# Decays of rows 512 to 1023 in two groups of two heads, the second group in z_a's last two products

## The chip, the cores and the metric

The kernel runs on one core of one Trainium2 chip. The metric is the device time in microseconds (us) of one execution. Before the change it is 1072.09 us, the median of 3 runs (1071.81 to 1072.77).

A core has engines that run side by side, each with a queue of its own that is worked off in order: TensorE (PE, matmuls into the PSUM banks), VectorE (DVE), ScalarE (ACT), GpSimd (POOL) and SyncE (SP, which here only issues DMAs). An instruction waits on semaphores for what other engines or DMAs have to finish first.

## The reference, cut to what matters

One layer of a decoder trunk on 1024 rows of width 1024: a norm, one wide projection cut into parts, gated linear attention with four heads, a gated short convolution, a merge and an output projection. The part that the change touches is the decay of the attention:

```python
proj = jnp.einsum('bsd,dc->bsc', h, w_in[i])
(q, k, v, z_a, gk_low, cb, cc, xc, z_c, g_a, g_c) = jnp.split(proj, idx, axis=-1)
gk = jax.nn.log_sigmoid((jnp.einsum('bsr,rk->bsk', gk_low, w_gk2[i]) + b_gk[i]).astype(jnp.float32)) / GATE_NORMALIZER
...
b = jnp.cumsum(gk, axis=3)
b_last = b[:, :, :, -1:, :]
q_in = q * jnp.exp(b)
k_in = k * jnp.exp(-b)
k_dec = k * jnp.exp(b_last - b)
decay = jnp.exp(b_last[:, :, :, 0, :])
...
y_a = jnp.einsum('bsv,vd->bsd', o * jax.nn.silu(z_a), w_branch_a[i])
```

## The kernel before

**Products.** Each large matrix product is done by a scheme with seven products of half-size blocks instead of eight, in float32 split into a high and a low part; each block product is three matmuls, hi x hi, lo x hi and hi x lo. The projections of v and of z_a are made by `wide`: here six products, in the order 3, 1, 2, 5, 4, 6. Each runs over four k-tiles `kt` and four row blocks `b`, three matmuls a time: 48 matmuls of 128x512, which add into four PSUM banks. Product 3 goes into the set X, product 1 into V, product 2 into Y, product 5 into V, products 4 and 6 into Y again. For z_a, X and Y are the banks m4, m5, o, o, and V is m0 to m3 (for v it is the other way round, so m0 to m3 are free for z_a's V once v's last results have been read). In the names, zaX, zaV and zaY are these banks; za1hi and za1lo are the weights of product 1, h1hi and h1lo its rows; zas, zau and sz are results on their way to the silu and to the store szd.

After product 5, DVE adds V to the copies zau (this frees V's banks); after product 4 it adds Y to the copies zas, before product 6 adds to the same banks.

**Decays.** `low_rank` makes the gate's low-rank rows for one half of the rows; `decays` then makes per head one matmul zp of 128x512 into a bank, reads it twice on ACT (Relu into a tile c, Abs into a tile t), then takes Exp and Ln of t on ACT (these, and the silu, need different function tables, so ACT_TABLE_LOAD stands between them), adds c on DVE, sums along the rows with a scan, subtracts the last row of each chunk, and stores both (ccd and cdd). A small Exp (dcs) and a product (dds) give the chunk's decay. The tiles t and c have four buffers each, which `quarter_sums` uses as well, for tiles named qs that are stored to tqd and loaded back later as turned0.

For the half that the change concerns (rows 512 to 1023), `more` runs `decays` for four heads and then `quarter_sums`; it is woven into z_a's products (`weave`, `tick`): after every second row block the generator is asked for its next step. `weights`, which prepares later weights (wt, wtd), is woven in beside it.

**What sets the order.** The program is recorded first and then put in order, engine by engine, by a list scheduler with costs of its own and due times. Matmuls of the main products keep their order; zp and the low-rank matmuls are side work that the scheduler slots in. `hurry` makes an instruction's due time earlier, `apart` asks for a distance from what it depends on. All instructions are issued from one line (L508), so views of the profile are read by the names of the tiles.

Of the kernel before, what the change touches and what calls it, by code (L numbers as in the profile page):

```python
# [9 lines left out]
F32 = mybir.dt.float32  # L10
# [509 lines left out]
def kernel(  # L520
# [42 lines left out]
    bgk = vec[:, 0:4]  # L563
# [8 lines left out]
    def dram(name, *shape):  # L572
        return dr.tile([P, *shape], F32, name=name)
# [5 lines left out]
    cd = [[[dram(f"c{w}d{h}_{i}", HALF) for w in "cd"] for i in range(2)] for h in range(H)]  # L579
# [16 lines left out]
    store = nc.sync.dma_start  # L596
# [6 lines left out]
    def mm(*a, **kw):  # L603
        nc.tensor.matmul(*a, skip_group_check=True, **kw)
# [12 lines left out]
    def weave(gen, after=1):  # L617
        woven.append([after, gen])
# [11 lines left out]
    def finish_woven():  # L630
        while woven:
            tick()
# [334 lines left out]
    def pairs(cs):  # L967
        for c in cs:
            c.prods = [k for k in PAIR if k in c.prods]
        return [list(cs[n:n + 2]) for n in range(0, len(cs), 2)]  # L970

    def run_groups(groups, more=(), ahead=6):


        todo = line_up(groups)
        seq = todo + line_up(more)
        for n, (c, k) in enumerate(todo):
            for reach, what in ((RING + ahead, "load"), (RING - 1, "prep")):
# [498 lines left out]
    with phase("v", [ph["prep0"]]) as qp:  # L1477
# [14 lines left out]
        smask = qp.tile([P, HALF], F32, name="smask")  # L1492
# [17 lines left out]
        nbgk = qp.tile([P, 4], F32, name="nbgk")  # L1510
# [20 lines left out]
                tt(low[a:a + 32], lowp[a:a + 32], f(low[a:a + 32]), op=ALU.subtract)  # L1531
            lows[half] = low

        def decays(half, tags):
            t1 = [qp.tile([P, HALF], F32, tag="t1", name=f"t1_{half}{h}", bufs=4) for h in range(H)]
            c = [qp.tile([P, HALF], F32, tag="c4", name=f"c4_{half}{h}", bufs=4) for h in range(H)]
            for h in range(H):
                zp = pso.tile([P, 512], F32, tag=tags[h], name=f"zp{half}_{h}", bufs=2 if tags[h] == "o" else 1)
                cs = slice(h * P, (h + 1) * P)
                nc.apart = 1.0  # L1540
                mm(zp, g2[:, cs], lows[half], start=True, stop=True)
                nc.apart, nc.hurry = 0.0, 6.0
                act(c[h], zp, AF.Relu, scale=-1.0, bias=nbgk[:, h:h + 1])
                act(t1[h], zp, AF.Abs, bias=bgk[:, h:h + 1])
                nc.hurry = 0.0
                yield 1
            for t in t1:
                act(t, t, AF.Exp, scale=-1.0)
            for t in t1:
                act(t, t, AF.Ln, bias=1.0)  # L1550
            yield 1
            by = lambda t: t.rearrange("p (n c t) -> p n c t", c=2, t=CH)
            for h in range(H):
                tt(t1[h], t1[h], c[h], op=ALU.add)
                nc.vector.tensor_tensor_scan(c[h], smask, t1[h], 0.0, op0=ALU.mult, op1=ALU.add)
                store(cd[h][half][0], c[h])
                last = by(c[h])[:, :, :, CH - 1]
                tt(by(t1[h]), by(c[h]), by(c[h])[:, :, :, CH - 1:CH].to_broadcast([P, NP, 2, CH]), op=ALU.subtract)
                store(cd[h][half][1], t1[h])
# [44 lines left out]
        def extra():  # L1604
            low_rank(0)
            yield 2
            yield from decays(0, ("o",) * 4)
            low_rank(1)

        def more():  # L1610
            yield from decays(1, ("m0", "m1", "m2", "m3"))
            yield from quarter_sums(1)

        wide("v", [wv[0, n] for n in range(4)], v_cons, ("m0", "m1", "m2", "m3"), ("o", "o", "m4", "m5"),
             [(ep, "ev", 3)] * 2, [(ep, "ev", 3), (qp, "t1", 4)], begun, lambda: weave(extra(), 1))
        weave(more(), 1)
        weave(weights(qp, pieces[:3], 3, 5.0), 2)
        wide("za", [wv[1, n] for n in range(4)], z_cons, ("m4", "m5", "o", "o"), ("m0", "m1", "m2", "m3"),
             [(qp, "vhi", 2)] * 2, [(qp, "vlo", 2)] * 2)
        finish_woven()  # L1620
        qks = []
        for hp in range(2):
# [367 lines left out]
    with phase("late", [ph["sw"], ep]) as lp:  # L1990
# [57 lines left out]
        with phase("fin", [ph["sw4"]], lp) as gp:  # L2048
# [152 lines left out]
            last = pairs(gts)  # L2201
# [74 lines left out]
```

## Time and profile before

| | us |
|---|---|
| median of 3 runs | 1072.09 |
| profiled execution | 1072.38 |
| its span | 1070.5 |
| mean granted clock of TensorE | 0.998 of full speed |

The span runs from the first to the last record of the profiled execution; 1.9 us lie around it. Times of instructions are microseconds from the start of the span. z_a's first product begins near 168, its second at 178.26, product 2 at 191.16, product 5 at 202.04 and product 4 at 212.92 in the chain of work that ended last (the chain counts a piece from the release of its first instruction; the timeline of PE has starts some 0.16 us earlier). After product 6, at 234.68, the cells of q and k begin (q0V, k0V, q0X, k0X).

How to read the rows: a row of the timeline has the start, the length, the engine, the line, the operation, what it writes and reads, and in brackets how long the engine stood idle before it, with the releaser. PE's matmuls overlap: one of 0.39 us follows the other after 0.23 us. A row of the windows has busy time per engine, with the number of instructions, then the granted clock, the DMA share and GB/s.

### The profile page before, as it was taken

To read this page: it belongs to the slowest core of one execution; us is meant where nothing else is said; L and a number is where in the kernel's file an instruction comes from. 1 tells how busy PE (TensorE), PEld (TensorE's weight loads), DVE (VectorE), ACT (ScalarE), POOL (GpSimd) and SP (SyncE) were. 2 spreads that over 40 slices of the span, in tenths; PEclk is the share of its full clock that TensorE was granted. 3 is DMA by queue.
4 is the path that set the end of the run, shared out by engine and by line. 5 is a ranking of instruction groups with operands and counts; after the bars stand their busy time and mean duration, and the time that the engine had idled before them with its cause. 6 is when DMAs were issued, how large, how long until landed. Compare 5 with 4: busy or idle time off the path is not lost.

```text
span 1070.5 us, 15921 instructions
## 1 busy us (share of the span) xinstructions
PE 1059.7 (99%) x5175; PEld 896.3 (84%) x5175; DVE 917.5 (86%) x1553; ACT 662.8 (62%) x1241; POOL 45.4 (4%) x83
## 2 busy tenths in 40 slices
PE   9999999999999999999999999999999999999996
PEld 7888887888888888888888888888888888888886
DVE  6889768977997888889889788887999879889896
ACT  6866689856654544566556376765856635466555
POOL 0000000000000000000000011110000000012021
PEclk9999999999999999999999999999999999999999
DMA  9985578785867443654557779978586779799973
GB/s 313 330 316 174 187 231 307 260 285 200 257 213 244 154 152 130 215 173 154 197 180 243 247 241 346 324 275 322 199 305 229 284 220 312 244 328 337 300 235 133
DMA packets 166979, 262.06 MB, mean 245 GB/s; under 512 B 14448, under 2 KB 79728, under 8 KB 163952
## 3 DMA queue, kind: packets, MB, share of 16 engines
q1 hardware_dynamic: 166752, 260.79, 72.1%
q8 instruction: 40, 0.66, 0.2%
q14 instruction: 43, 0.35, 0.1%
q10 hardware_dynamic: 144, 0.26, 0.1%
HBM read 168.72 MB, written 92.27 MB: 244 GB/s over the span
## 4 chain that ended last, share of the span: by engine, by line
PE 98%; ACT 1%; DMA 1%; DVE 0%; issue 0%; SPq 0%; POOL 0%; POOLq 0%; ACTq 0%
PE vY L508 3%; PE zaY L508 3%; PE vV L508 2%; PE op L508 2%; PE zaV L508 2%; PE pe L508 2%; PE zaX L508 1%; PE vzV L508 1%; PE vzX L508 1%; PE kv L508 1%; PE ga1Y L508 1%; PE ga0Y L508 1%; PE k0Y L508 1%; PE zc2Y L508 1%; PE zc1Y L508 1%; PE ga2Y L508 1%
## 5 line engine op out<-in xcount | busy, mean ns | idle before, releaser
L508 DVE TENSOR_TENSOR wt<-wt 128x256 f32<-128x256 f32 x64 | 26.9, 420 | 2.2 <-DMA wtd<-wt 1.9
L508 ACT ACT_TABLE_LOAD x20 | 25.7, 1283 | 1.1 <-PEq L2265 0.7
L508 DVE SCALAR_TENSOR_TENSOR u<-t,vec,u 128x512 f32<-128x512 f32 x32 | 23.8, 747 | 2.6 <-ACT u L508 2.5
L508 ACT ACTIVATE junk<-x 128x512 bf16<-128x512 f32 (+1 forms) x30 | 18.0, 600 | 12.0 <-DVE x L508 11.7
L508 POOL MEMSET t<- 128x2 f32 x8 | 0.8, 100 | 410.3 <-ACT kk L508 206.5
L508 POOL TENSOR_SCALAR rg<-ms 128x1 f32<-128x1 f32 x8 | 6.4, 798 | 261.6 <-ACT junk L508 261.4
L508 ACT ACTIVATE u<-t,vec 128x512 f32<-128x512 f32 x16 | 11.6, 726 | 7.9 <-issue 4.6
L508 ACT ACTIVATE junk<-op 128x256 bf16<-128x256 f32 x32 | 12.2, 380 | 3.8 <-PE op L508 3.7
L508 ACT ACTIVATE wt<-wt,vec 128x256 f32<-128x256 f32 x32 | 13.6, 497 | 1.0 <-DMA wt<-in_wb_dram 1.0
L508 ACT ACTIVATE og<-op,or 128x256 f32<-128x256 f32 x32 | 13.3, 470 | 1.2 <-POOL or L508 1.1
L508 ACT CAST S<-S 128x512 fp32r<-128x512 f32 x14 | 8.6, 617 | 8.7 <-PE op L508 7.5
L508 PE MATMUL pe<-wpehi,pThi 128*128 128x512 f32 x32 | 12.7, 398 | 0.6 <-ACT pThi L508 0.5
L508 ACT ACTIVATE oq<-oq,vec 128x512 f32<-128x512 f32 x20 | 13.1, 715 | 0.0
L508 PE MATMUL op<-v,aTh 128*128 128x256 f32 x64 | 12.8, 283 | 0.0
L508 PE MATMUL pe<-wpelo,pThi 128*128 128x512 f32 x32 | 12.7, 398 | 0.0
L508 DVE TENSOR_TENSOR szl<-og,szl 128x512 f32<-128x512 f32 x16 | 11.0, 687 | 2.0 <-ACT og L508 2.0
L508 PE MATMUL pe<-wpehi,pTlo 128*128 128x512 f32 x32 | 12.1, 393 | 0.0
L508 POOL TENSOR_TENSOR or<-or,mhalf 128x2 f32<-128x2 f32 x16 | 11.9, 746 | 1.3
L508 DVE SCALAR_TENSOR_TENSOR hq<-hq,vec,rt 128x512 f32<-128x512 f32 x16 | 11.4, 741 | 0.0
L508 DVE TENSOR_TENSOR s<-y,s 128x512 f32<-128x512 f32 x16 | 11.0, 686 | 0.5 <-ACT s L508 0.5
L508 POOL TENSOR_SCALAR or<-oms 128x2 f32<-128x2 f32 x16 | 5.6, 348 | 137.6 <-ACT junk L508 137.6
L508 DVE TENSOR_TENSOR x<-x,pe 128x512 f32<-128x512 f32 (+1 forms) x18 | 11.2, 629 | 0.3
(3671 smaller groups left out, 4333.7 us busy)
## 6 DMA issues: line engine op xcount, KB each, us to landing
wtd<-wt SPq DMA_DIRECT2D x88, 128.0 KB, 2.7
wt<-in_wb_dram SPq DMA_DIRECT2D x16, 512.0 KB, 4.5
v<-vd SPq DMA_DIRECT2D x16, 512.0 KB, 5.9
wgq<-wtd SPq DMA_DIRECT2D x7, 1024.0 KB, 6.6
qk<-qkd SPq DMA_DIRECT2D x12, 512.0 KB, 6.0
vraw<-in_wv_dram SPq DMA_DIRECT2D x20, 256.0 KB, 3.3
zaraw<-in_wv_dram SPq DMA_DIRECT2D x20, 256.0 KB, 4.4
uq<-ud SPq DMA_DIRECT2D x5, 1024.0 KB, 6.9
```

Of the source, the lines that this page charges most:

```text
L508: o.call(*[place(a) for a in o.args], **{k: place(a) for k, a in o.kw.items()})
```

## The change

`decays` now takes the heads that it is to make, and loops over them. `more` makes heads 0 and 1 only, in the banks m0 and m1, and then the quarter sums. Heads 2 and 3 are made by a second generator, in the banks m2 and m3, which z_a's `wide` starts by its hook `late`: after the weights of product 6 have been prepared and before the matmuls of product 4 are recorded. The hook was there before (v's `wide` uses it); z_a's did not use it.

```diff
-        def decays(half, tags):
-            t1 = [qp.tile([P, HALF], F32, tag="t1", name=f"t1_{half}{h}", bufs=4) for h in range(H)]
-            c = [qp.tile([P, HALF], F32, tag="c4", name=f"c4_{half}{h}", bufs=4) for h in range(H)]
-            for h in range(H):
-                zp = pso.tile([P, 512], F32, tag=tags[h], name=f"zp{half}_{h}", bufs=2 if tags[h] == "o" else 1)
+        def decays(half, heads, tags):
+            t1 = [qp.tile([P, HALF], F32, tag="t1", name=f"t1_{half}{h}", bufs=4) for h in heads]
+            c = [qp.tile([P, HALF], F32, tag="c4", name=f"c4_{half}{h}", bufs=4) for h in heads]
+            for n, h in enumerate(heads):
+                zp = pso.tile([P, 512], F32, tag=tags[n], name=f"zp{half}_{h}", bufs=2 if tags[n] == "o" else 1)
...
-            for h in range(H):
-                tt(t1[h], t1[h], c[h], op=ALU.add)
+            for n, h in enumerate(heads):
+                tt(t1[n], t1[n], c[n], op=ALU.add)
...
-                yield from decays(0, ("o",) * 4)
+                yield from decays(0, range(4), ("o",) * 4)
...
         def more():
-            yield from decays(1, ("m0", "m1", "m2", "m3"))
+            yield from decays(1, range(2), ("m0", "m1"))
             yield from quarter_sums(1)
...
         wide("za", [wv[1, n] for n in range(4)], z_cons, ("m4", "m5", "o", "o"), ("m0", "m1", "m2", "m3"),
-             [(qp, "vhi", 2)] * 2, [(qp, "vlo", 2)] * 2)
+             [(qp, "vhi", 2)] * 2, [(qp, "vlo", 2)] * 2, None, lambda: weave(decays(1, range(2, 4), ("m2", "m3")), 1))
```

No matmul is added or taken away: PE has 5000 rows in both orders, with the same operations. ACT has four rows more, which are table loads (24 for 20 in the program). What follows are three places in the order; zp_2 and zp_3 are the matmuls of heads 2 and 3, and the number behind a name is that of a buffer.

**Place 1: from product 3 to product 1 of z_a, on PE.** Before, ending in the first matmuls of zaV:

```order
L508 MATMUL zaX_1748<-za3hi_1822,h3lo 128x512
L508 MATMUL zp_2_1984<-low_1742,g_1407 128x512
L508 MATMUL zaX_1784<-za3hi_1822,h3hi 128x512
L508 MATMUL zaX_1784<-za3lo_1847,h3hi 128x512
L508 MATMUL zaX_1784<-za3hi_1822,h3lo 128x512
L508 MATMUL zaX_1815<-za3hi_1822,h3hi 128x512
L508 MATMUL zaX_1815<-za3lo_1847,h3hi 128x512
L508 MATMUL zaX_1815<-za3hi_1822,h3lo 128x512
L508 MATMUL zaV_2000<-za1hi_1864,h1hi 128x512
L508 MATMUL zp_3_2004<-low_1742,g_1407 128x512
L508 MATMUL zaV_2000<-za1lo_1880,h1hi 128x512
L508 MATMUL zaV_2000<-za1hi_1864,h1lo 128x512
```

and in the changed kernel:

```order
L508 MATMUL zaX_1669<-za3hi_1763,h3lo 128x512
L508 MATMUL zaX_1775<-za3hi_1763,h3hi 128x512
L508 MATMUL zaX_1775<-za3lo_1830,h3hi 128x512
L508 MATMUL zaX_1775<-za3hi_1763,h3lo 128x512
L508 MATMUL zaX_1843<-za3hi_1763,h3hi 128x512
L508 MATMUL zaX_1843<-za3lo_1830,h3hi 128x512
L508 MATMUL zaX_1843<-za3hi_1763,h3lo 128x512
L508 MATMUL zaV_1990<-za1hi_1795,h1hi 128x512
L508 MATMUL zaV_1990<-za1lo_1851,h1hi 128x512
L508 MATMUL zaV_1990<-za1hi_1795,h1lo 128x512
L508 MATMUL zaV_1999<-za1hi_1795,h1hi 128x512
```

Both zp are gone from here; zaV follows on zaX.

**Place 2: the first row blocks of product 4, on PE and on ACT.** PE before, the third and fourth row block:

```order
L508 MATMUL zaY_2044<-za4lo_2220,h4hi 128x512
L508 MATMUL zaY_2044<-za4hi_2204,h4lo 128x512
L508 MATMUL zaY_2048<-za4hi_2204,h4hi 128x512
L508 MATMUL zaY_2048<-za4lo_2220,h4hi 128x512
L508 MATMUL zaY_2048<-za4hi_2204,h4lo 128x512
L508 MATMUL zaY_2062<-za4hi_2204,h4hi 128x512
L508 MATMUL zaY_2062<-za4lo_2220,h4hi 128x512
L508 MATMUL zaY_2062<-za4hi_2204,h4lo 128x512
```

and now:

```order
L508 MATMUL zaY_2022<-za4hi_2167,h4hi 128x512
L508 MATMUL zaY_2022<-za4lo_2190,h4hi 128x512
L508 MATMUL zaY_2022<-za4hi_2167,h4lo 128x512
L508 MATMUL zaY_2031<-za4hi_2167,h4hi 128x512
L508 MATMUL zp_2_2372<-low_1747,g_1407 128x512
L508 MATMUL zaY_2031<-za4lo_2190,h4hi 128x512
L508 MATMUL zaY_2031<-za4hi_2167,h4lo 128x512
L508 MATMUL zp_3_2378<-low_1747,g_1407 128x512
L508 MATMUL zaY_2081<-za4hi_2167,h4hi 128x512
L508 MATMUL zaY_2081<-za4lo_2190,h4hi 128x512
L508 MATMUL zaY_2081<-za4hi_2167,h4lo 128x512
```

zp_2 stands behind the first matmul of zaY's third block, zp_3 behind its last. On ACT, what stood between the last cast of product 6's weights (za6hi) and the casts of q0 and k0 before:

```order
L508 CAST za6hi_2385<-zaT_1695 128x512
L508 CAST qs12h<-qs_2345 128x512
L508 ACT_TABLE_LOAD
L508 ACTIVATE zau_2258<-zau_2258 128x512
L508 ACTIVATE zau_2270<-zau_2270 128x512
L508 CAST q0hi<-q0T_2431 128x512
```

and now:

```order
L508 CAST za6hi_2359<-zaT_1703 128x512
L508 ACT_TABLE_LOAD
L508 ACTIVATE zau_2229<-zau_2229 128x512
L508 ACTIVATE t_12_2380<-zp_2_2372,vec 128x512
L508 ACTIVATE c_12_2387<-zp_2_2372,nbgk 128x512
L508 ACTIVATE t_13_2393<-zp_3_2378,vec 128x512
L508 ACTIVATE c_13_2398<-zp_3_2378,nbgk 128x512
L508 ACT_TABLE_LOAD
L508 ACTIVATE t_12_2380<-t_12_2380 128x512
L508 ACTIVATE t_13_2393<-t_13_2393 128x512
L508 ACT_TABLE_LOAD
L508 ACTIVATE t_12_2380<-t_12_2380 128x512
```

The reads of zp_2 and zp_3, two Exp and two Ln, with two more table loads, (the second Ln, of t_13, follows the last row shown) stand between the first zau's silu and the second's.

**Place 3: from product 4 to the cells of q and k, on DVE and on SP.** DVE before, around the sums zas that free zaY's banks for product 6:

```order
L508 TENSOR_TENSOR q0lo<-q0T_2431,q0hi 128x512
L508 TENSOR_TENSOR k0lo<-k0T_2437,k0hi 128x512
L508 TENSOR_TENSOR zas_2120<-zaY_2039,zas_2120 128x512
L508 TENSOR_TENSOR zas_2134<-zaY_2044,zas_2134 128x512
L508 TENSOR_TENSOR zas_2167<-zaY_2048,zas_2167 128x512
L508 TENSOR_TENSOR q0lo<-q0raw_2261,q0hi 128x512
L508 TENSOR_TENSOR zas_2172<-zaY_2062,zas_2172 128x512
```

and now:

```order
L508 TENSOR_TENSOR wt_1_0_2356<-wt_1_0_2356 128x256 x4
L508 TENSOR_TENSOR t_12_2380<-t_12_2380,c_12_2387 128x512
L508 TENSOR_TENSOR t_13_2393<-t_13_2393,c_13_2398 128x512
L508 TENSOR_TENSOR zas_2110<-zaY_2013,zas_2110 128x512
L508 TENSOR_TENSOR zas_2118<-zaY_2022,zas_2118 128x512
L508 TENSOR_TENSOR zas_2124<-zaY_2031,zas_2124 128x512
L508 TENSOR_TENSOR zas_2135<-zaY_2081,zas_2135 128x512
L508 SCALAR_TENSOR_TENSOR c_12_2387<-smask,t_12_2380 128x512
L508 SCALAR_TENSOR_TENSOR c_13_2398<-smask,t_13_2393 128x512
L508 TENSOR_TENSOR t_12_2380<-c_12_2387 128x512
L508 TENSOR_TENSOR t_13_2393<-c_13_2398 128x512
```

The adds t_12 and t_13 come ahead of the four zas, their scans (SCALAR_TENSOR_TENSOR c_12, c_13) behind them. SP before, the loads that k0X and q0X read:

```order
L508 DMA q1raw_2513<-in_wc_dram 128x512
L508 DMA szd_0_2429<-zau_2253 128x512
L508 DMA turned0h<-tqd_1h 128x512
L508 DMA turned0l<-tqd_1l 128x512
L508 DMA turned0h<-tqd_2h 128x512
L508 DMA turned0l<-tqd_2l 128x512
L508 DMA turned0h<-tqd_0h 128x512
L508 DMA turned0l<-tqd_0l 128x512
L508 DMA k1raw_2580<-in_wc_dram 128x512
L508 DMA szd_1_2587<-sz_0_1_2576 128x512
L508 DMA szd_1_2587<-sz_0_2_2583 128x512
```

and now:

```order
L508 DMA szd_0_2384<-zau_2215 128x512
L508 DMA szd_0_2384<-zau_2222 128x512
L508 DMA k1raw_2559<-in_wc_dram 128x512
L508 DMA szd_1_2567<-sz_0_0_2552 128x512
L508 DMA szd_1_2567<-sz_0_1_2561 128x512
L508 DMA turned0h<-tqd_1h 128x512
L508 DMA turned0l<-tqd_1l 128x512
L508 DMA turned0h<-tqd_2h 128x512
L508 DMA turned0l<-tqd_2l 128x512
L508 DMA turned0h<-tqd_0h 128x512
L508 DMA turned0l<-tqd_0l 128x512
L508 DMA szd_1_2567<-sz_0_2_2572 128x512
```

The loads turned0 stood behind the last store of zau; now two stores of sz stand between.

More of the change, by code (lines that the diff above doesn't have):

```diff
@@ L1542, in decays @@
                 nc.apart, nc.hurry = 0.0, 6.0
-                act(c[h], zp, AF.Relu, scale=-1.0, bias=nbgk[:, h:h + 1])
-                act(t1[h], zp, AF.Abs, bias=bgk[:, h:h + 1])
+                act(c[n], zp, AF.Relu, scale=-1.0, bias=nbgk[:, h:h + 1])
+                act(t1[n], zp, AF.Abs, bias=bgk[:, h:h + 1])
                 nc.hurry = 0.0
@@ L1552, in decays @@
             by = lambda t: t.rearrange("p (n c t) -> p n c t", c=2, t=CH)
-            for h in range(H):
-                tt(t1[h], t1[h], c[h], op=ALU.add)
[L1555 to L1559, printed above, removed]
+            for n, h in enumerate(heads):
+                tt(t1[n], t1[n], c[n], op=ALU.add)
+                nc.vector.tensor_tensor_scan(c[n], smask, t1[n], 0.0, op0=ALU.mult, op1=ALU.add)
+                store(cd[h][half][0], c[n])
+                last = by(c[n])[:, :, :, CH - 1]
+                tt(by(t1[n]), by(c[n]), by(c[n])[:, :, :, CH - 1:CH].to_broadcast([P, NP, 2, CH]), op=ALU.subtract)
+                store(cd[h][half][1], t1[n])
                 dc = dcs[:, h, half]
```

## The prediction

> **What bounds the kernel now.** First the page: busy shares, the chain that ended last, and the dearest group that this change multiplies.
>
> ```profile
> PE 1059.7 (99%) x5175; PEld 896.3 (84%) x5175; DVE 917.5 (86%) x1553; ACT 662.8 (62%) x1241; POOL 45.4 (4%) x83
> ...
> PE 98%; ACT 1%; DMA 1%; DVE 0%; issue 0%; SPq 0%; POOL 0%; POOLq 0%; ACTq 0%
> ...
> L508 ACT ACT_TABLE_LOAD x20 | 25.7, 1283 | 1.1 <-PEq L2265 0.7
> ```
>
> TensorE (PE) is busy for 99% of the span and is 98% of the chain. A change that leaves the matmuls alone, as this one does, can only win back PE's waits. The view of PE's waits lists them all:
>
> ```profile
> PE zaV L508 <- ACT t L508: 1.2, 2, 1.0
> PE warm L508 <- DVE zero L508: 1.0, 1, 1.0
> PE pe L508 <- ACT pThi L508: 0.5, 1, 0.5
> ```
>
> Two of the three belong to the start. The only one in the steady state is zaV waiting for ACT's t, 1.2 us. The timeline of PE there, then of ACT, then DVE's last vlo, then a piece of the chain:
>
> ```profile
> 179.49 0.40 PE L508 MATMUL zaV<-za1hi,h1lo 128*128 128x512 f32 x1
> 180.86 0.50 PE L508 MATMUL zaV<-za1hi,h1hi 128*128 128x512 f32 x1 [0.98 <-ACT t L508]
> 181.20 0.40 PE L508 MATMUL zaV<-za1lo,h1hi 128*128 128x512 f32 x1
> 181.44 0.40 PE L508 MATMUL zaV<-za1hi,h1lo 128*128 128x512 f32 x1
> 182.02 0.51 PE L508 MATMUL zaV<-za1hi,h1hi 128*128 128x512 f32 x1 [0.18 <-ACT t L508]
> 182.36 0.40 PE L508 MATMUL zaV<-za1lo,h1hi 128*128 128x512 f32 x1
> ...
> 174.04 0.68 ACT L508 ACTIVATE t<-zp,vec 128x512 f32<-128x512 f32 x1
> ...
> 178.08 1.58 ACT L508 ACTIVATE sz<-zaX 128x512 f32<-128x512 f32 x3
> 179.53 0.70 ACT L508 ACTIVATE c<-zp,nbgk 128x512 f32<-128x512 f32 x1
> 180.10 0.71 ACT L508 ACTIVATE t<-zp,vec 128x512 f32<-128x512 f32 x1
> 180.67 0.72 ACT L508 ACTIVATE c<-zp,nbgk 128x512 f32<-128x512 f32 x1
> 181.24 0.73 ACT L508 ACTIVATE t<-zp,vec 128x512 f32<-128x512 f32 x1
> ...
> 177.06 0.68 DVE L508 TENSOR_TENSOR vlo<-vY,vhi 128x512 fp32r<-128x512 f32 x1
> ...
> 202.04 10.88 PE zaV L508 x48
> ```
>
> 48 matmuls take 10.88 us, so a step is 0.2267 us. Four steps here are longer: 1.37 (179.49 to 180.86), 0.34, 0.58 (181.44 to 182.02) and 0.34. Their sum, 2.63, less four plain steps, 0.91, is **1.72 us**: the wait and the slow restart behind it. The cause stands in ACT's rows. Row blocks 2 and 3 of zaV go to banks m2 and m3, which hold zp1_2 and zp1_3 until ACT's second read of each (180.10 and 181.24) ends, and ACT gets there only after three silus.
>
> **What the change removes.** In the new order zp1_2 and zp1_3 are gone from this place. Heads 0 and 1 use m0 and m1, and ACT has read those by 174.7 (174.04). Next late is DVE's last vlo (177.06; it frees m3), done at 177.7, while PE wants m3 near 180: over 2 us spare, and the orders of ACT and DVE ahead of it hardly change. So **-1.72 us**, to which nothing can be added, since PE waits nowhere else after the start. PE's rows keep their number, so each later point lies 1.72 us earlier, and between here and the two moved matmuls 2.17 (less two steps).
>
> **First cost: the moved matmuls on PE.** They now stand inside product 4's first rows, zp1_2 behind 7 of its matmuls. The rows of before that carry this part (PE, DVE, ACT, and two windows, where the third pair is DVE's busy time):
>
> ```profile
> 212.76 0.39 PE L508 MATMUL zaY<-za4hi,h4hi 128*128 128x512 f32 x1
> ...
> 223.64 0.39 PE L508 MATMUL zaY<-za6hi,h6hi 128*128 128x512 f32 x1
> ...
> 188.57 0.69 DVE L508 TENSOR_TENSOR t<-t,c 128x512 f32<-128x512 f32 x1 [1.08 <-ACT t L508]
> ...
> 204.08 1.22 DVE L508 TENSOR_TENSOR_SCAN c<-smask,t 128x512 f32<-128x512 f32 x1
> 205.21 0.67 DVE L508 TENSOR_TENSOR za4lo<-zaraw,za4hi 128x512 fp32r<-128x512 f32 x1
> ...
> 216.18 0.42 DVE L508 TENSOR_TENSOR wt<-wt 128x256 f32<-128x256 f32 x1
> 216.51 0.69 DVE L508 TENSOR_TENSOR zau<-zaV,zau 128x512 f32<-128x512 f32 x1
> ...
> 221.99 1.88 DVE L508 TENSOR_TENSOR zas<-zaY,zas 128x512 f32<-128x512 f32 x3
> ...
> 187.91 0.63 ACT L508 ACTIVATE t<-t 128x512 f32<-128x512 f32 x1
> ...
> 196.45 1.28 ACT L508 ACT_TABLE_LOAD   x1
> 197.74 0.22 ACT L508 ACTIVATE dcs<-c 128x8 f32<-128x8 f32 x1
> ...
> 212.61 0.62 ACT L508 CAST qs13h<-qs 128x512 fp32r<-128x512 f32 x1 [1.75 <-DVE qs L508]
> 215.41 0.62 ACT L508 CAST za6hi<-zaT 128x512 fp32r<-128x512 f32 x1 [2.18 <-DVE zaT L508]
> ...
> 180.00:185.00 5.00, 3.96 (x16) 2.97 (x17) 2.54 (x5) 5.00 (x11) 0.00 (x0) 1.00 0.56 187
> 185.00:190.00 5.00, 5.00 (x24) 4.14 (x23) 3.54 (x6) 4.94 (x8) 0.00 (x0) 1.00 0.79 250
> ```
>
> Product 4 starts at 212.76 - 2.17 = 210.59, so zp1_2 is due at 210.59 + 7 x 0.2267 = 212.2. It needs m2, which DVE's first zau reads, at 216.51 before. PE's queue runs in order, so all of product 4 would stand behind it. When is that zau now? Steps on DVE are 0.60 (221.99: three in 1.88, the last 0.69), 1.13 for a scan (204.08 to 205.21) and 0.33 for a half tile (216.18 to 216.51). DVE's anchor is the first add t<-t,c, held at 188.57 by ACT's Ln of 187.91. Ahead of that Ln ACT loses four reads of zp (4 x 0.57), two small dcs (0.12 each), and a silu, a copy and a cast that now stand behind it (about 0.5 each): 4.1 us. The anchor moves to 184.5. From there to the zau DVE had 27.9 us without a wait. It loses two scans, four full rows and three halves (5.65), and gains four full rows, a half and a dds (2.8): 25.1 us. On the way it now waits for ACT three times (two dcs, one Ln), by my count of ACT's steps 1.5 us together. So zau begins at 211.1, ends at 211.8, and the matmul at 212.2 does **not wait: 0**, with 0.4 us to spare. From the other side: if all 3.9 us that DVE idles in the two windows stay (2.46 and 1.46), zau begins at 216.51 - 3.6 (the net work that left its front since the stage began) = 212.9 and ends at 213.6: a wait of 1.4 and 0.1 for the restart. I take 0 and keep 1.5.
>
> **Second cost: the banks of zaY.** Product 6 adds to the banks that zas reads on DVE after product 4 (221.99 before, with PE's first use at 223.64). In the new order DVE has two adds of t_12 and t_13 ahead of the four zas, and these wait for ACT's Ln. Queued behind them stand the zas, then two scans, then q0lo and k0lo, which PE wants only after product 6. ACT's line up to it: the last za6hi waits for the last matmul of product 5 to free its buffer, so it begins at 210.8; then 0.62; a table load with its gaps (196.45 to 197.74, and 0.02 ahead: 1.31); one silu 0.5 (178.08: three in 1.58); four reads of zp 4 x 0.57; load 1.31; two Exp 1.1 to the end; load 1.31; two Ln, the first ending 0.63 on. That is Ln at 219.5, its end at 220.1; the two adds on DVE 1.2; the first zas from 221.3 to 222.0. PE wants the bank at 223.64 - 2.17 + 2 x 0.2267 = 221.92. So PE waits 0.1 to 0.15, and a restart cost 0.11 above (0.34 against 0.23): **+0.27**. The other three zas follow at 0.60 each while PE wants one per 0.68. The line hangs on PE itself, so it moves with PE; a wait in the first cost shifts PE but hardly ACT, and swallows this one: the two count as the larger, not as a sum. The 12 steps are good to about 0.3, so 0 to 0.6.
>
> [...]
>
> **Third cost: SP's queue.** The six loads turned0 stood right behind a store of zau. Now they stand behind the stores of two of z_a's last silus:
>
> ```profile
> 229.37 0.32 SPq L508 DMA_DIRECT2D turned0h<-tqd_1h  x1
> 231.81 0.43 SPq L508 DMA_DIRECT2D turned0l<-tqd_0l  x1
> ...
> DMA to landing us min/median/max: 5.3/5.6/6.0
> ...
> L508 PE MATMUL q0X<-turned0h,q0k00Shi x2: 281/281/281, 244.1 to 244.5; 128*128 128x256 f32 x2
> ...
> 232.68 1.96 ACT L508 ACTIVATE sz<-zaY 128x512 f32<-128x512 f32 x3 [0.23 <-PE zaY L508]
> ```
>
> The second of these silus ends at 232.68 + 0.5 + 0.65 = 233.8, or up to 1.45 us sooner with PE. Issue of the loads runs then from about 233.7 to 236.2 (2.44 us for six) and landing from 239.0 to 242.2. PE wants the last two for q0X, from 244.1 - 1.45 = 242.65: 0.4 to spare, which may just be missed; the first four are wanted by k0X, whose 12 steps of 0.12 stand ahead, so they have more. Bounds 0 and 1.5 (SP held once more by a landing); I take **+0.2**, near the row's own 5.3 to 6.0.
>
> **At nothing:** 9.6 us of ACT's work (four reads, four Exp and Ln, two dcs, three or four loads) move into 212 to 235. ACT has room there: its ten gaps from 207.5 to 232.0 add up to 11.6 us, with those of 212.61 and 215.41 among the largest. Without that room the third cost grows one for one. DVE's two scans and four rows go behind zas; the next matmuls that need DVE stand a whole product, 10.88 us, later. Heads 2 and 3 take their four stores of ccd and cdd along, on SP from 199 to 207 to about 226: four issues of 0.3 to 0.4 us ahead of the silus' stores, in a queue that waits for those silus anyway. Only the cells of the second pair of heads read them. lowp1's block moves four matmuls forward in v, where PE has no wait.
>
> Sum: -1.72 + 0.27 + 0.2 = -1.25. The profiled execution, 1072.38, becomes 1071.1. It was 0.29 above the median of 1072.09, so in runs **1070.8**.
>
> **Rivals.**
> 1. *No new wait.* Both waits are within the error of my steps. Gain 1.72: 1070.4. Against it: a margin of -0.1 us at product 6.
> 2. *The wait only moves, to zp1_2 or to turned0l.* The first at its bound costs 1.5, the second 1.5: net -0.4 to +0.3, about 1072. For it: PE and DVE have queues in order there, and 0.4 us is little. Against: the DVE sum above.
> 3. *Slower: the zas stand behind a late Ln.* One mechanism: ACT reaches the last za6hi late, since it still waits for DVE as in rows 212.61 and 215.41 (1.75 and 2.18 us); Ln, adds, zas and product 6 follow one for one. 3.93 late gives -1.45 + 3.93 = +2.5, 1074.6. It decides from 1.45 us of lateness on. Against: DVE's zaT is now due near 206, four us before PE frees the buffer. [...]
> 4. *The stall stays:* something else holds m2 or m3 at 180. Net 0 to +0.5 (the new costs), 1072.3. Against: the 2 us spare at m3.
>
> **Chances.** Forecast (1070.5 to 1071.4) 0.46; rival 1 0.22; rival 2 0.18; rival 3 0.09; rival 4 0.05. About 0.2%, 2.1 us, is what a measurement of this kernel can tell from no change. The gain can't exceed 1.72, so faster needs a lucky pair of medians: 0.05. Slower by 0.2% needs rival 3 at nearly its full price: 0.07. The same: 0.88. For 8 in 10 the range runs from a full gain and 0.4 us of scatter in the runs, 1070.0, to rival 2 and rival 4 with the same scatter, 1072.8.
>
> **What would show it.** zaV's steps at 178 to 182 all 0.23 (right); zp1_2's start near 212.2 with or without "<-DVE zau"; the first zas near 221.3 and PE's first product 6 matmul near 222.1, marked "<-DVE zas"; ACT_TABLE_LOAD x24 at 1283 ns with the next start 1.3 us on; turned0 landing by 242.7. A gap above 0.6 us at product 6, a load with a longer shadow, or a stall left at 180 proves a step wrong. The granted clock should stay at 1.00, as it did behind the old wait (the last column but two of the windows).

## The result, and the profile after

| | before | after |
|---|---|---|
| median of 18 runs each, taken together | 1072.34 | 1070.74 (1070.25 to 1072.13) |
| profiled execution | 1072.38 | 1070.41 |
| its span | 1070.5 | 1068.3 |

The ratio after to before is 0.9985, with a 95% interval of 0.9978 to 0.9992: the change saves about 1.6 us, which lies under the 0.2% bound of the chances, though the interval leaves out 1. The page has the same matmuls and four more table loads, as forecast:

```profile
PE 1058.7 (99%) x5175; PEld 896.6 (84%) x5175; DVE 918.3 (86%) x1553; ACT 666.6 (62%) x1245; POOL 45.3 (4%) x83
...
L508 ACT ACT_TABLE_LOAD x24 | 30.8, 1283 | 1.2 <-PEq L2265 0.7
```

The view of PE's waits, complete:

```profile
PE warm L508 <- DVE zero L508: 1.0, 1, 1.0
PE pe L508 <- ACT pThi L508: 0.5, 1, 0.5
```

The row of zaV is gone and none has come in its place. That view drops waits of a tenth or two, so PE's timeline was read at the four places of the prediction: zaV's third row block, zp_2, product 6, and q0X's first two rows.

```profile
178.93 0.39 PE L508 MATMUL zaV<-za1hi,h1lo 128*128 128x512 f32 x1
179.15 0.39 PE L508 MATMUL zaV<-za1hi,h1hi 128*128 128x512 f32 x1
...
211.11 0.40 PE L508 MATMUL zaY<-za4hi,h4hi 128*128 128x512 f32 x1
211.35 0.39 PE L508 MATMUL zp<-low,g 128*128 128x512 f32 x1
...
220.91 0.39 PE L508 MATMUL zaY<-za4hi,h4lo 128*128 128x512 f32 x1
221.32 0.47 PE L508 MATMUL zaY<-za6hi,h6hi 128*128 128x512 f32 x1
221.63 0.39 PE L508 MATMUL zaY<-za6lo,h6hi 128*128 128x512 f32 x1
...
241.88 0.28 PE L508 MATMUL q0X<-turned0h,q0k00Shi 128*128 128x256 f32 x1
241.99 0.28 PE L508 MATMUL q0X<-turned0l,q0k00Shi 128*128 128x256 f32 x1
```

Starts 0.23 us apart are plain steps for 512 columns, 0.12 for 256. Only product 6 has longer ones: 0.41 and 0.31, which is 0.27 over two plain steps. DVE and ACT at zau, at the line with Ln, and at zas:

```profile
210.12 1.28 DVE L508 TENSOR_TENSOR zau<-zaV,zau 128x512 f32<-128x512 f32 x2
...
219.27 1.29 DVE L508 TENSOR_TENSOR t<-t,c 128x512 f32<-128x512 f32 x2 [2.37 <-ACT t L508]
220.48 2.48 DVE L508 TENSOR_TENSOR zas<-zaY,zas 128x512 f32<-128x512 f32 x4
...
217.31 1.28 ACT L508 ACT_TABLE_LOAD   x1
218.61 1.15 ACT L508 ACTIVATE t<-t 128x512 f32<-128x512 f32 x2
```

DVE stands idle for 2.37 us until ACT's first Ln is through, adds, and reaches zas at 220.48. The first zas ends about 221.17, 0.03 us after PE is due at product 6 (220.91 and a plain step), and PE starts there at 221.32. SP's issue of the last turned0 load, and the view of DMA issues with its time from issue to landing as the last number:

```profile
235.77 0.43 SPq L508 DMA_DIRECT2D turned0l<-tqd_0l  x1
...
turned0l<-tqd_0l SPq DMA_DIRECT2D x1, 256.0 KB, 6.1
```

It lands 6.06 us after its issue in the trace, at 241.82; q0X reads it at 241.99.

**Where the span's 2.26 us went.** The spans (1070.5 and 1068.3) are not compared whole: the first 21 us, ahead of anything that the change touches, differ by 0.63 us between these two executions, and by up to 0.84 among the 13 profiled in this study. From the matmul records I therefore take one **stretch**: from the start of TensorE's 81st matmul (ms<-ones,sq, near 21) to that of its 1501st (cc0V<-h5lo,cc0hi, near 330). It is 310.22 us before and 308.61 after: **-1.61**, against -1.60 for the medians. What lies behind the stretch is 738.87 to 738.96 us in 12 of the 13 executions and 738.46 in the other.

### The profile page after: what moved, and what is told of

Its sections match the earlier page's. It is cut to its first block, busy times and chain, and to the rows that moved or that the text cites. A ratio compares the mean times of both kernels' runs of the same rounds, so it can differ in the third digit from the quotient of the medians.

```text
span 1068.3 us, 15924 instructions
## 1 busy us (share of the span) xinstructions
PE 1058.7 (99%) x5175; PEld 896.6 (84%) x5175; DVE 918.3 (86%) x1553; ACT 666.6 (62%) x1245; POOL 45.3 (4%) x83
## 4 chain that ended last, share of the span: by engine, by line
PE 98%; ACT 0%; DMA 0%; DVE 0%; issue 0%; POOL 0%; POOLq 0%; SPq 0%
PE zaY L508 3%; PE vY L508 3%; PE pe L508 2%; PE zaV L508 2%; PE vV L508 2%; PE op L508 2%; PE zaX L508 1%; PE vzV L508 1%; PE vzX L508 1%; PE kv L508 1%; PE ga1Y L508 1%; PE ga0Y L508 1%; PE k0Y L508 1%; PE cc3Y L508 1%; PE zc1Y L508 1%; PE cc1Y L508 1%
## 5 line engine op out<-in xcount | busy, mean ns | idle before, releaser
L508 ACT ACT_TABLE_LOAD x24 | 30.8, 1283 | 1.2 <-PEq L2265 0.7
L508 DVE TENSOR_TENSOR wt<-wt 128x256 f32<-128x256 f32 x64 | 27.0, 423 | 3.2 <-DMA wtd<-wt 2.1
L508 DVE SCALAR_TENSOR_TENSOR u<-t,vec,u 128x512 f32<-128x512 f32 x32 | 23.9, 753 | 2.6 <-ACT u L508 2.5
L508 ACT ACTIVATE junk<-x 128x512 bf16<-128x512 f32 (+1 forms) x30 | 18.0, 600 | 12.0 <-DVE x L508 11.7
L508 POOL MEMSET t<- 128x2 f32 x8 | 0.8, 99 | 408.6 <-DMA qkd<-qd 204.5
L508 POOL TENSOR_SCALAR rg<-ms 128x1 f32<-128x1 f32 x8 | 6.4, 796 | 261.6 <-ACT junk L508 261.4
L508 ACT ACTIVATE u<-t,vec 128x512 f32<-128x512 f32 x16 | 11.6, 726 | 8.2 <-issue 4.6
L508 ACT ACTIVATE junk<-op 128x256 bf16<-128x256 f32 x32 | 12.1, 379 | 3.8 <-PE op L508 3.7
L508 ACT ACTIVATE wt<-wt,vec 128x256 f32<-128x256 f32 x32 | 13.6, 497 | 1.0 <-DMA zc2raw<-in_wc_dram 1.0
L508 ACT ACTIVATE og<-op,or 128x256 f32<-128x256 f32 x32 | 13.3, 469 | 1.2 <-POOL or L508 1.1
L508 ACT CAST S<-S 128x512 fp32r<-128x512 f32 x14 | 8.6, 618 | 8.7 <-PE op L508 7.5
L508 ACT ACTIVATE oq<-oq,vec 128x512 f32<-128x512 f32 x20 | 13.1, 715 | 0.0
L508 PE MATMUL pe<-wpehi,pThi 128*128 128x512 f32 x32 | 12.6, 394 | 0.5 <-ACT pThi L508 0.5
L508 PE MATMUL pe<-wpelo,pThi 128*128 128x512 f32 x32 | 12.8, 400 | 0.0
L508 PE MATMUL op<-v,aTh 128*128 128x256 f32 x64 | 12.8, 283 | 0.0
L508 DVE TENSOR_TENSOR szl<-og,szl 128x512 f32<-128x512 f32 x16 | 11.0, 687 | 2.0 <-ACT og L508 2.0
L508 PE MATMUL pe<-wpehi,pTlo 128*128 128x512 f32 x32 | 12.0, 390 | 0.0
L508 POOL TENSOR_TENSOR or<-or,mhalf 128x2 f32<-128x2 f32 x16 | 11.9, 745 | 1.3
L508 DVE SCALAR_TENSOR_TENSOR hq<-hq,vec,rt 128x512 f32<-128x512 f32 x16 | 11.5, 746 | 0.0
L508 DVE TENSOR_TENSOR x<-x,pe 128x512 f32<-128x512 f32 (+1 forms) x18 | 11.2, 632 | 0.3
L508 DVE TENSOR_TENSOR s<-y,s 128x512 f32<-128x512 f32 x16 | 11.0, 686 | 0.5 <-ACT s L508 0.5
L508 DVE STREAM_TRANSPOSE oT<-szl 128x512 f32<-128x512 f32 x16 | 11.3, 706 | 0.1
```

Source lines behind the costliest of these rows:

```text
L508: o.call(*[place(a) for a in o.args], **{k: place(a) for k, a in o.kw.items()})
```

## The experiments

split_only and all_late change the generators. Each of the other edits moves or repeats a few recorded instructions after the scheduler has put them in order, so that all other rows stay where they were; read_first does this to the kernel before, the rest to the changed kernel. In the edits, `at` finds a recorded instruction by its engine and name, and `behind` puts one right behind another. The line of the issuing loop then has another number (L517 to L523 for L508). The table has all of them; a median is of 11 runs, but of 18 before and after and of 5 in all_late. A ratio is to the runs of before that were made with that kernel.

| kernel | median, us | ratio, 95% interval | stretch, us |
|---|---|---|---|
| before | 1072.34 | | 310.22 |
| split_only | 1072.42 | 1.0003 (0.9994 to 1.0012) | 310.19 |
| read_first | 1071.89 | 0.9995 (0.9987 to 1.0004) | 309.80 |
| after | 1070.74 | 0.9985 (0.9978 to 0.9992) | 308.61 |
| zau_late | 1071.77 | 0.9995 (0.9987 to 1.0004) | 309.38 |
| ln_late2 | 1071.87 | 0.9997 (0.9988 to 1.0006) | 309.80 |
| ln_late4 | 1074.18 | 1.0018 (1.0009 to 1.0027) | 312.72 |
| zas_first | 1070.96 | 0.9990 (0.9981 to 0.9999) | 308.72 |
| turned_late | 1071.19 | 0.9989 (0.9980 to 0.9998) | 309.47 |
| turned_early | 1071.48 | 0.9992 (0.9983 to 1.0001) | 309.09 |
| both | 1071.12 | 0.9990 (0.9981 to 0.9999) | 309.63 |
| k1raw_behind | 1070.27 | 0.9983 (0.9974 to 0.9992) | 308.34 |
| all_late | 1078.58 | 1.0061 (1.0048 to 1.0074) | 316.61 |

### split_only and read_first: is the stall what the gain comes from?

split_only has the two groups, but runs both at the start, where the four heads were.

```diff
             yield from decays(1, range(2), ("m0", "m1"))
+            yield from decays(1, range(2, 4), ("m2", "m3"))
             yield from quarter_sums(1)
```

(and z_a's `wide` without the hook.)

> Two groups of two heads as in the changed kernel, but the second started right behind the first in z_a's first products, as before. The scheduler makes of it the very order of before on PE, ACT, DVE and SP, so this is also the kernel before run again. My theory: 1072.3, the wait at zaV as before. It shows besides how much the first 22 us differ from one profile to the next; in the two profiles so far they differ by 0.6 us ahead of any changed row, and I expect such a scatter again. Rival (the splitting in the program text matters): 1070.7.

The scheduler's order comes out the same as before on every engine, so this is the kernel before run once more: 1072.42, stretch 310.19. Splitting alone does nothing, and two profiles of one order differ by 0.03 us in the stretch.

read_first leaves the heads where they were, and puts ACT's four reads of zp_2 and zp_3 behind the first of the three silus instead of behind all three.

```diff
+        last = at(PE, [o.name for o in order if o.engine == PE and o.name.startswith("zp1_3")][0])
+        for n in (2, 1):
+            behind([o for o in order if o.engine == ACT and o.name.startswith(f"sz0_0_{n}<-zaX")][0], last)
+        for n in (3, 2):
+            behind(at(ACT, [o.name for o in order if o.name.startswith(f"t1_1{n}<-zp")][0]), last)
+            behind(at(ACT, [o.name for o in order if o.name.startswith(f"c4_1{n}<-zp")][0]), last)
```

> The kernel before with one thing else: on ACT the four reads of zp1_2 and zp1_3 stand behind the first of the three silus sz<-zaX instead of behind all three; every other row is the same, and the zp stay where they were. My theory (zaV waits only since ACT reaches the reads after three silus): the reads end near 179.9 and 181.05 instead of 180.8 and 182.0, PE's two waits shrink from 0.98 and 0.18 to 0.25 and 0.3 with a restart each; loss 0.8 instead of 1.72, time 0.9 under before, about 1071.4. Rival (the change's gain is not from this wait): no change from before, 1072.3.

PE's timeline at zaV and at product 6:

```profile
179.47 0.40 PE L521 MATMUL zaV<-za1hi,h1lo 128*128 128x512 f32 x1
179.88 0.50 PE L521 MATMUL zaV<-za1hi,h1hi 128*128 128x512 f32 x1
...
222.42 0.39 PE L521 MATMUL zaY<-za4hi,h4lo 128*128 128x512 f32 x1
222.80 0.47 PE L521 MATMUL zaY<-za6hi,h6hi 128*128 128x512 f32 x1
```

The step at zaV's third block shrinks from 1.37 to 0.41; with its three other long steps (0.33, 0.59 and 0.34) 0.76 us is lost there instead of 1.72. So ACT's second reads, late behind the silus, are what held zaV. Half of that gain is lost again: product 6, where PE now comes earlier against DVE, shows two small waits (steps of 0.38 and 0.31 at its first row block, 0.38 and 0.34 at its fourth, together 0.50 over plain steps). The stretch gains 0.42.

### zau_late: the spare at zp_2, and "the larger, not the sum"

DVE makes q0T and k0T twice, ahead of the first zau.

```diff
+        twice = at(DVE, "q0T1<-q0raw1,q0raw0"), at(DVE, "k0T1<-k0raw1,k0raw0")
...
+                for _ in range(1 if o in twice else 0):
+                    o.call(*[place(a) for a in o.args], **{k: place(a) for k, a in o.kw.items()})
```

> The changed kernel with two rows more on DVE (q0T1 and k0T1 are made twice, 1.2 us) ahead of the first zau. In the trace that zau (the one that frees m2) ends at 210.8 and zp_2 starts at 211.35, 0.5 us later. My theory: zp_2 waits to 212.05, 0.7 us and 0.1 of restart; ACT's line to Ln hangs on product 5 and hardly moves, so the wait at product 6 vanishes: the larger of the two counts, +0.8 - 0.27 = +0.5 on the changed kernel, about 1071.2. Rival (the two add up, as ACT moves with zp): +0.8, 1071.5. Second rival (DVE has more room than the trace shows): 0, 1070.7.

DVE's zau, then PE at zp_2 and at product 6:

```profile
211.50 1.28 DVE L518 TENSOR_TENSOR zau<-zaV,zau 128x512 f32<-128x512 f32 x2
...
211.09 0.39 PE L518 MATMUL zaY<-za4hi,h4hi 128*128 128x512 f32 x1
212.24 0.50 PE L518 MATMUL zp<-low,g 128*128 128x512 f32 x1 [0.77 <-DVE zau L518]
212.58 0.40 PE L518 MATMUL zaY<-za4lo,h4hi 128*128 128x512 f32 x1
...
221.92 0.39 PE L518 MATMUL zaY<-za4hi,h4lo 128*128 128x512 f32 x1
222.15 0.39 PE L518 MATMUL zaY<-za6hi,h6hi 128*128 128x512 f32 x1
```

zau starts 1.38 us later than in the changed kernel, and zp_2, due at 211.32, starts 0.92 late: 1.38 - 0.92 = 0.46 us was the spare. The steps 1.15 and 0.34 cost 1.04 us. Product 6 then waits for nothing, its step is plain, and the stretch grows by 0.77, which is 1.04 - 0.27. A wait in front swallows the one behind it, where that one hangs on an engine (ACT, DVE) that the first doesn't delay.

### ln_late2 and ln_late4: what a later Ln costs

ACT copies t_12 onto itself two or four times ahead of the first Ln of the second group.

```diff
+        slow = at(ACT, "t1_12<-t1_12", 1)
...
+                for _ in range(2 if o is slow else 0):
+                    self.tc.nc.scalar.copy(place(o.args[0]), place(o.args[0]))
```

> The changed kernel with two copies more on ACT (t_12 onto itself) ahead of the first Ln of the second group, 0.52 us each; the order on all engines is otherwise that of the changed kernel. My theory (Ln, add, zas and product 6 follow one for one): the wait at product 6 grows from 0.18 to 1.2 us, time +1.0 on the changed kernel, about 1071.8. Rival (ACT's and DVE's time there is hidden, since both idle in that stretch): +0, 1070.7.

> As the run before with four copies, 2.1 us. My theory: wait at product 6 of 2.3 us, +2.1 on the changed kernel, about 1072.8: slower than before by 0.5. Rival (hidden): 1070.7. A slope of less than one would say that something else gives way, for example the table load that then stands idle.

PE's timeline of ln_late2 at product 6:

```profile
222.99 0.47 PE L518 MATMUL zaY<-za6hi,h6hi 128*128 128x512 f32 x1 [1.18 <-DVE zas L518]
```

With two copies, the steps at product 6 are 1.57 and 0.31: a loss of 1.43 instead of 0.27, which is 1.16 more (1.19 in the stretch). ACT's Ln starts at 220.28 instead of 218.61, 1.67 later, of which 0.51 is this execution's later start (its 81st matmul is that much later): 1.16, one for one. With four copies PE's timeline shows something else besides the wait, and the windows (granted clock: third number from the end of a row) say what:

```profile
221.71 0.39 PE L518 MATMUL zaY<-za4hi,h4lo 128*128 128x512 f32 x1
224.58 0.47 PE L518 MATMUL zaY<-za6hi,h6hi 128*128 128x512 f32 x1 [2.48 <-DVE zas L518]
...
225.59 0.58 PE L518 MATMUL zaY<-za6lo,h6hi 128*128 128x512 f32 x1
...
229.22 0.40 PE L518 MATMUL zaY<-za6lo,h6hi 128*128 128x512 f32 x1
...
225.50:226.00 0.50, 0.50 (x4) 0.36 (x3) 0.50 (x2) 0.50 (x2) 0.00 (x0) 0.63 0.00 0
226.00:228.50 2.50, 2.50 (x7) 1.97 (x6) 2.50 (x4) 2.50 (x5) 0.00 (x0) 0.50 0.68 238
...
229.00:229.50 0.50, 0.50 (x4) 0.41 (x3) 0.50 (x2) 0.50 (x1) 0.00 (x0) 0.96 1.08 356
```

The wait's two steps cost 2.73. Then, 1 us after PE has resumed, its clock falls to half for 3.4 us: the nine steps from 225.59 to 229.22 take 3.63 instead of 2.04, another 1.59. Together 4.32, less the 0.27 of before: 4.05 of the 4.11 us that the stretch grows. So the mechanism of rival 3 holds (Ln, adds, zas, product 6 one for one), and the longer wait, with its half clock, cost more than one for one.

### zas_first, turned_late: who stands behind product 6's wait?

zas_first puts the two adds behind the four zas on DVE; turned_late puts the six turned0 loads behind one more store of sz on SP.

```diff
+        def behind(o, other):
+            order.remove(o)
+            order.insert(order.index(other) + 1, o)
...
+        last = max((at(DVE, f"zas{b}<-zaY{b},zas{b}") for b in range(4)), key=order.index)
+        behind(at(DVE, "t1_13<-t1_13,c4_13"), last)
+        behind(at(DVE, "t1_12<-t1_12,c4_12"), last)
```

> The changed kernel with one thing else: on DVE the adds t_12 and t_13 stand behind the four zas instead of ahead of them; every other row on every engine is the same. My theory (the wait of 0.18 us that PE still has, and 0.09 of restart, at the start of product 6 come from the zas queued behind adds that wait for Ln): the step into product 6 falls from 0.41 + 0.31 to 0.23 + 0.23, the zas start near 220.0 instead of 220.5, gain 0.27 us on the changed kernel, about 1070.5, or 1.9 under before. Rival (PE waits there for za6hi or za6lo, not for zas): the step stays at 0.41 and the time at 1070.7. Second rival (the scans, now 1.2 us later, hold up ccd, cdd or q0lo): a new wait of up to 1 us at q0V, 1071.5.

```diff
+        loads = [o for o in order if o.engine == SP and o.name.startswith("turned0")][:6]
+        last = [o for o in order if o.engine == SP and o.name.endswith("<-sz1_0_2")][0]
+        for o in reversed(loads):
+            behind(o, last)
```

> The changed kernel with one thing else: on SP the six loads turned0 stand behind one store of sz more. In the trace of the changed kernel the last of them lands at 241.8 and its first reader on PE (the second row of q0X) is due at 242.05, so 0.2 us are spare. My theory: the loads are issued 0.5 later and land 0.5 later, PE waits 0.3 to 0.5 with its restart at q0X, +0.4 on the changed kernel, 1071.1. Rival (there is more room, for example since landing is spaced by the load of the DMA engines): 0, 1070.7. Second rival (SP is held by the landing that its ring waits for): +1 to +2, 1072.

PE's timeline of zas_first, at product 6 and at q0X:

```profile
221.58 0.39 PE L518 MATMUL zaY<-za4hi,h4lo 128*128 128x512 f32 x1
221.81 0.39 PE L518 MATMUL zaY<-za6hi,h6hi 128*128 128x512 f32 x1
...
242.28 0.28 PE L518 MATMUL q0X<-turned0h,q0k00Shi 128*128 128x256 f32 x1
242.69 0.39 PE L518 MATMUL q0X<-turned0l,q0k00Shi 128*128 128x256 f32 x1
```

and of turned_late at q0X:

```profile
242.07 0.39 PE L519 MATMUL q0X<-turned0h,q0k00Shi 128*128 128x256 f32 x1
242.73 0.39 PE L519 MATMUL q0X<-turned0l,q0k00Shi 128*128 128x256 f32 x1 [0.28 <-DMA turned0l<-tqd_0l]
```

In zas_first product 6 waits no more, which shows that the two adds ahead of zas were its whole cost. But q0X's second row, 0.12 behind the first in the changed kernel, now comes 0.41 behind it: PE is 0.27 earlier against SP, and the last load isn't: counted from the 81st matmul it is issued 0.53 later than in the changed kernel and lands 0.15 later, though its row and those ahead of it on SP are the same. So about half of this wait comes from PE being early, and half from the later landing in this one profile. With the step behind it, 0.22 instead of 0.12, that loses 0.39, and the stretch is 308.72, 0.11 longer than without the edit. In turned_late the last load is issued at 236.43 instead of 235.77, and lands after 6.26 us instead of 6.06, at 242.69; PE reads it 0.04 later. So the changed kernel's spare (241.82 to 241.99) is 0.13 with these 0.04 taken off. It covers that much of the 0.66 and 0.20, and q0X's second row starts 0.74 later, at 242.73. Past 0.1 us a later load delays PE about one for one (stretch +0.86, with a small wait of 0.21 at k0X's turned0l too).

### both, turned_early, k1raw_behind: can the 0.27 be had?

both is zas_first with the six loads ahead of the first two sz stores; turned_early has the second edit alone.

```diff
+        sp = [o for o in order if o.engine == SP]
+        stop = sp[sp.index(loads[0]) - 3]
+        for o in reversed(loads):
+            behind(o, stop)
```

> The changed kernel with two moves: the adds t_13 and t_12 stand behind the four zas (as in zas_first), and the six turned0 loads stand on SP ahead of the first two sz stores, so that they needn't wait for the silus and for 0.9 us of issues. My theory (the spare of the turned0 loads at q0X is 0.2 us, and once product 6 waits no more, q0X waits 0.28 us): the loads are issued about 1 us sooner, neither product 6 nor q0X waits, and the time is 0.27 us under the changed kernel's, about 1070.45 us, ratio 0.9983; no step over 0.3 us between zp and q0X in TensorE's row. Rival 1 (the loads share the DMA engines with the raw loads and the sz stores, and land no sooner when issued sooner): q0X still waits about 0.3 us, 1070.75. Rival 2 (the delayed sz stores hold a buffer of ScalarE's next silus): a wait appears in ScalarE's row behind sz and at q0V or k0V, over 1071.

> The changed kernel with the turned0 move alone. My theory: q0X did not wait in the changed kernel, so nothing is gained, 1070.74 within the scatter, and product 6 still loses 0.27 us (steps of about 0.41 and 0.31). Rival (some of the loss behind product 6 came from SP): 1070.4 or less, with product 6 the same.

In both, neither product 6 nor turned0l holds PE, but two new rows stand among PE's waits; SP's waits from 225 to 243 and its timeline show where they come from:

```profile
PE q0X L523 <- ACT q0u L523: 0.2, 1, 0.2
PE q0Y L523 <- DVE q0s L523: 0.2, 1, 0.2
...
SPq L523 <- DMA szd<-sz: 4.2, 1, 4.2
...
242.29 0.32 SPq L523 DMA_DIRECT2D c<-ccd  x1
```

SP waits 4.2 us for a store of sz to land before it issues the load c<-ccd, at 242.29; in the changed kernel that load went out at 237.87. The kernel's text says why: the tiles sz and c are made by the same helper `ev`, with three buffers, so the load of c waits until the second store of sz has read its buffer. It goes out 0.02 us after that store's landing in the changed kernel too (237.85), and here the store was issued later (236.40, not 232.71). Behind its wait SP issues one transfer right after the other up to the next c<-ccd, at 245.50 (243.46 in the changed kernel, whose times here are 0.50 earlier throughout). The chain runs over that second load, which lands at 251.79, to ACT's and DVE's work on q, and PE waits at 254.31 (0.51 lost), 265.64 (0.43) and once more at q1Y near 303.7 (0.24). The stretch is 1.02 longer than the changed kernel's. None of the three theories had this; rival 2 had the right stores, but looked for the wait on ACT. turned_early shows it alone: q0Y is late by 0.36, the stretch +0.48, and product 6 loses its 0.27 as ever.

k1raw_behind therefore leaves the sz stores where they are and moves a load that nobody wants soon, k1raw, behind the six.

```diff
+        k1raw = sp[sp.index(loads[0]) - 3]
+        behind(k1raw, loads[-1])
```

> The changed kernel with the adds t_13 and t_12 behind the four zas (as in zas_first), and one SP row moved: k1raw<-in_wc_dram stands behind the six turned0 loads instead of ahead of the two sz stores. The stores of sz stay where they are, so nothing is put between them and c<-ccd, which is what waited in 'both'. My theory: the turned0 loads are issued up to 0.5 us sooner against TensorE's row, q0X's wait of 0.28 us goes, product 6 waits no more, and the time is 0.27 us under the changed kernel's, about 1070.45 us, ratio 0.9983. Rival 1 (SP waits for the silus there and not for its own issues: the loads start when the second sz is made, whatever stands ahead): q0X waits as in zas_first, 1070.75 or more. Rival 2 (k1raw, 2.9 us later, is late at its first reader q1k10S at about 247.5): DVE shows a wait of DMA k1raw there, and TensorE waits behind it, over 1071.

PE's timeline at product 6 and q0X, SP's last load and its landing:

```profile
221.29 0.39 PE L522 MATMUL zaY<-za4hi,h4lo 128*128 128x512 f32 x1
221.52 0.39 PE L522 MATMUL zaY<-za6hi,h6hi 128*128 128x512 f32 x1
...
242.00 0.28 PE L522 MATMUL q0X<-turned0h,q0k00Shi 128*128 128x256 f32 x1
242.11 0.28 PE L522 MATMUL q0X<-turned0l,q0k00Shi 128*128 128x256 f32 x1
...
235.84 0.43 SPq L522 DMA_DIRECT2D turned0l<-tqd_0l  x1
...
turned0l<-tqd_0l SPq DMA_DIRECT2D x1, 256.0 KB, 5.9
```

Both steps are plain, the load lands at 241.72 (5.87 us after its issue), 0.39 ahead of PE, and no longer step follows in the stretch. The stretch is 308.34, 0.27 under the changed kernel's, and the median of 11 runs 1070.27. By the stretch, of one profile each, this is the best of the versions; the intervals of the two ratios overlap, so the runs alone do not show it.

### all_late: all four heads at the hook

```diff
-            yield from decays(1, range(2), ("m0", "m1"))
...
-             [(qp, "vhi", 2)] * 2, [(qp, "vlo", 2)] * 2, None, lambda: weave(decays(1, range(2, 4), ("m2", "m3")), 1))
+             [(qp, "vhi", 2)] * 2, [(qp, "vlo", 2)] * 2, None, lambda: weave(decays(1, range(4), ("m0", "m1", "m2", "m3")), 1))
```

> All four heads of rows 512 to 1023 in one group, started by the hook before product 4, with zp in m0 to m3; the quarter sums alone stay in front. The scheduler has made a new order: four zp inside product 4's first 14 rows, 24 table loads, on DVE the adds and the zas by turns (zas, add, zas, add, zas, zas). My theory: the wait at zaV goes as in the changed kernel (-1.8); at product 6 ACT has eight reads and three Exp ahead of Ln, so the third and fourth zas stand behind an add that waits for Ln near 222 and PE waits 0 to 0.8: 1070.5 to 1071.3. Rival (it is the grouping in twos that gains, since four heads make ACT's line 4 us longer): wait of about 4 us, 1074.

It costs 8.0 us in the stretch; neither the theory nor the rival had that much. PE's timeline, ACT's, and the windows:

```profile
235.47 0.39 PE L508 MATMUL q0V<-h1hi,q0lo 128*128 128x512 f32 x1
241.21 0.79 PE L508 MATMUL k0V<-h1hi,k0hi 128*128 128x512 f32 x1 [5.35 <-ACT sz L508]
...
240.07 1.08 ACT L508 ACTIVATE sz<-zaY 128x512 f32<-128x512 f32 x2
...
238.50:239.00 0.50, 0.00 (x0) 0.00 (x0) 0.50 (x2) 0.48 (x3) 0.00 (x0) 0.73 0.00 0
239.00:245.50 6.50, 4.29 (x10) 3.43 (x11) 4.39 (x9) 4.15 (x7) 0.00 (x0) 0.50 0.75 204
245.50:246.00 0.50, 0.50 (x3) 0.39 (x3) 0.00 (x0) 0.00 (x0) 0.00 (x0) 0.94 0.72 246
```

k0V needs a bank that z_a's last silus read, and ACT reaches these only at 240.07, behind the casts, the small dcs and the table loads of four heads. The step of 5.74 us costs 5.51; the half clock behind it makes 11 steps take 4.63 instead of 2.49, another 2.14; product 6 has two steps that lose 0.51, in place of 0.27, and there PE waits for za6lo on DVE and not for zas. That is 7.9 of the 8.0. This is rival 3's kind of mechanism (ACT's line too long), at another bank than the one that I had named. The theory of this run, zas behind the adds at product 6, is not what cost the time.

## Why the prediction was right, step by step

- **The time: nearer than the working deserves.** The forecast saves 1.25 us from a median of 1072.09. The measured saving is 1.60, from a median of before that came out at 1072.34 in 18 runs. That 1070.8 and 1070.74 agree within 0.1 is luck: the two differences, 0.35 and 0.25, mostly cancel. Of the 0.35 by which the saving is larger, 0.2 is the third cost below and 0.1 the stall under "Missed".
- **-1.72 for the stall: right.** zaV's steps are all plain, and read_first shows that the two late reads caused it.
- **First cost, 0 with 0.4 to spare: right.** zp_2 doesn't wait. zau ends about 210.8 (two in 1.28 from 210.12), zp_2 starts at 211.35; zau_late measures the spare as 0.46.
- **Second cost, +0.27: the line is right, the exact size is luck.** zas stand behind the adds, which stand behind Ln; the loss is 0.27, and zas_first takes it away whole. But the prediction's own terms for ACT's line add up to an Ln at 219.2, not 219.5. With 219.2 the first zas ends at 221.75, ahead of PE's 221.92, and the forecast would have been no wait. The run has that earlier Ln (218.61, which is 219.24 when this execution's 0.63 us earlier start is added). It also has two things that the prediction did not: 0.15 us pass from the end of zas (221.17) to the matmul (221.32), and PE was due 0.15 earlier than forecast (221.14, with the 0.63 221.77). The slip of 0.27 in the sum stands in for these two. The 0 to 0.6 that the prediction gave to this cost held. That the two costs count as the larger is shown by zau_late.
- **Third cost, +0.2: a size too large.** It measured 0. The forecast's own spare was 0.4 "which may just be missed"; it is 0.1, and was not missed. turned_late and zas_first show that this term is real one step later: it is the next wait in line.
- **At nothing: right.** The stretch of the changed kernel has no long step besides those at product 6 and three small ones before 44 us that the kernel before has too. So the moved work on ACT and DVE, the later stores and the four more table loads cost PE nothing beyond the second cost.
- **The table loads: right.** 24 of them at 1283 ns, with the next start 1.3 us on, were forecast. The load is 1283 here, and the Ln behind the load of 217.31 starts at 218.61, 0.02 us after its end. A load stands between Exp and Ln of t in both traces; whether one table could serve both was not tried.
- **Missed:** PE of before had one more small stall, a step of 0.33 in product 6 of v (0.48 long at 156.75; split_only and read_first, with the same order there, have it too). It is gone after: -0.10. The sum with the measured terms is -1.72 - 0.10 + 0.27 = -1.55; the remaining 0.06 of -1.61 are steps a few ns longer or shorter. So the statement that nothing could be added to the 1.72 was off by a tenth: the waits view leaves out stalls that small.
- Of the rivals, 1 (no new wait) is what k1raw_behind makes of the change; 2 did not occur in the changed kernel, but zau_late and turned_late are its two halves; 3 (slower than before) needs four more copies on ACT: with two, product 6 waits 1.18 us and the stretch is still 0.42 under that of before; 4 did not occur.

## What to carry to other kernels

Where PE is busy for 99% of the time, take the gain from the long steps in its timeline at the place, and then ask at each later handover which engine is next late and by how much: here zaV, product 6 and q0X's turned0l stood in a row, each within a few tenths of the one ahead. A wait that is taken away is worth only what the next handover has to spare (zas_first: 0.27 taken away at product 6, 0.39 lost at q0X), and a wait ahead of another swallows it where the two hang on different engines (zau_late: 1.04 more at zp_2, 0.27 less at product 6). To make room for a load, move what nobody wants soon (k1raw), not what others queue behind (the sz stores, whose buffers the loads of c need: SP waited 4.2 us for one in both).

## What the runs showed of the hardware that was not expected

Waits of 1.0 (before) and 1.18 us (ln_late2) left the granted clock at 1.00; in ln_late4, with one of 2.48, and in all_late, with one of 5.35, it fell to 0.50. In ln_late4 the half clock came late: it began about 225.63, an estimate from the 0.63 of its window, when PE had been at work again for 1.0 us, and it ended about 229.04, estimated from the 0.96 of that window, 3.4 later. In all_late it began about 238.73, within the wait, and ended about 245.56 (from 0.73 and 0.94), 6.8 later. Why it came behind the one wait and within the other, these runs do not show. Whether a wait between 1.18 and 2.48 us would do was not tried, and the 1.18 us lay in one place only.
